# Norm factors put into the input rows before they are turned, with most turns behind the first products

## The chip, the cores and the metric

The kernel runs on one core of one Trainium2 chip. The metric is device time in microseconds (us) from the first to the last instruction of one execution, as a median of several runs; less is better. The engines are TensorE (PE in the profile; PEld is its weight load), VectorE (DVE), ScalarE (ACT), GpSimd (POOL) and SyncE (SP), which issues most transfers. A name with q (ACTq, SPq) is that engine's queue of DMA issues.

## The reference

One layer of a streaming encoder on 1024 prompt tokens and 32 sample tokens, width 1024: a SwiGLU feed-forward, a mix of two attention groups, a second SwiGLU. All inputs and outputs are 32-bit floats. What the change touches is the very beginning:

```python
def rms_norm(x, g):
    xf = x.astype(jnp.float32)
    y = xf * lax.rsqrt(jnp.mean(xf * xf, axis=-1, keepdims=True) + EPS)
    return (y * g.astype(jnp.float32)).astype(x.dtype)

def swiglu(x, w_in, w_out):
    a, b = jnp.split(x @ w_in, 2, axis=-1)
    return (jax.nn.silu(a) * b) @ w_out

x = x + 0.5 * swiglu(rms_norm(x, ffn1_norm), ffn1_w_in, ffn1_w_out)
```

`w_in` has 1024 rows and 2 x 2816 columns: a half for `a`, a half for `b`.

## The kernel before

Each 32-bit operand of a product is split into a high part (ScalarE, `split`, L158) and the rest that it leaves (VectorE, L159), and a product of two operands is three TensorE instructions per block of 128 rows: high by high, high by rest, rest by high. The names end in h and l: `B110h`, `B110l`; weights are `wh`, `wl`. The feed-forward is computed by Strassen's scheme with seven products per column block j of the weights, so sums of weights (`S1` to `S4`, `rS` before their split) and sums of tokens (`T1` to `T4`, `B11`, `B22`) are needed. The 1056 tokens stand in two groups c, of 256 and 272 in each half of the tokens; tiles 0, 1, 4, 5 of the input belong to c = 0, tiles 2, 3, 6, 7 and the sample's 8 to c = 1.

The input comes as tiles of 128 tokens by 1024 features (`xt`; `Tile`), and the products need features on the partitions, so each tile is turned, in two halves of four blocks. It is turned twice: once plainly, to be stored in a DRAM tensor `xf` for later (`raw`, L830; a copy `st` by ScalarE, L855, then a store), and once with its norm factor. For the factor, ScalarE squares and sums a tile (L815, into a spare buffer), GpSimd computes r from the sum (L817, L818), VectorE scales the identity by r into `dg` (L820), and TensorE multiplies the tile by `dg` (`normed`, L832). VectorE multiplies the result by the norm's gain g1 into `xn` (L843, L847 for the sample).

`early_products` then computes, for the first six column blocks (j = 0 to 5; `EARLY`), the two of the seven products that need only unsummed operands: for j = 0 and 1 first with c = 0, then with c = 1, and from j = 2 on both for each j. Their results go through `e` (L411 ScalarE, L413 VectorE) into a DRAM tensor `pd`, by stores that ScalarE issues. Between these groups it calls `amid(n)`, which holds turns, saves and preparations: `prep_first` and `prep_rest` (L383 and splits) build the token operands. A column's weights are split when the last product that reads their buffer is done.

The main loop (`first_products`) goes through all j; for j < 6 it has five products left and fetches the two others from `pd` (`p1`, and `gt` on which ScalarE then does a SiLU, L573). During one j, it loads the next j's weights, sums and splits them. SyncE and ScalarE's queue carry the loads; the stores of a finished j are `td` and `gd`.

A scheduler of the language sets the order of instructions on each engine by the order of the code, by readiness and by priorities; each engine then works its list in order. Where the code says `behind(g, ...)`, it adds an order after the named instructions. The first stretch of the program is that of TensorE's 72 plain turns, 144 records of turns by `dg`, and the early products of j = 0 and 1.

## Time and profile before

| | us |
|---|---|
| median of 3 runs | 2148.93 |
| lowest and highest | 2145.74, 2150.28 |
| the profiled execution | 2150.68 |
| its span, first to last instruction | 2149.0 |
| TensorE busy | 2107.0 |
| TensorE's first instruction | 7.64 |
| first early product | 19.10 |
| first product of j = 2 | 50.26 |
| first product of the main loop | 73.68 |

The profile is that of one execution. In the timeline a row has the start in us, the duration, engine, line, operation, output <- input, the number of instructions run together (x16), and in brackets the idle time of the engine before it with what ended that. In the groups, a row has the busy time, the mean of one in ns, and the idle time before. Duration of TensorE rows overlaps: the distance of two starts is what one costs. In the windows a row has the busy time of PE, PEld, DVE, ACT and POOL, with counts, then the granted TensorE clock (1.00 is full), the share of the DMA engines, and GB/s.

### The profile page before, as it was taken

To read this page: it belongs to the slowest core of one execution; us is meant where nothing else is said; L and a number is where in the kernel's file an instruction comes from. 1 tells how busy PE (TensorE), PEld (TensorE's weight loads), DVE (VectorE), ACT (ScalarE), POOL (GpSimd) and SP (SyncE) were. 2 spreads that over 40 slices of the span, in tenths; PEclk is the share of its full clock that TensorE was granted. 3 is DMA by queue.
4 is the path that set the end of the run, shared out by engine and by line. 5 is a ranking of instruction groups with operands and counts; after the bars stand their busy time and mean duration, and the time that the engine had idled before them with its cause. 6 is when DMAs were issued, how large, how long until landed. Compare 5 with 4: busy or idle time off the path is not lost. (4 is left out here: it accounts for less than half of the span.)

```text
span 2149.0 us, 41522 instructions
## 1 busy us (share of the span) xinstructions
PE 2107.0 (98%) x16331; PEld 2053.9 (96%) x16331; DVE 1471.8 (68%) x2559; ACT 936.1 (44%) x1830; POOL 582.7 (27%) x873
## 2 busy tenths in 40 slices
PE   8999999999999999999999999999999999999999
PEld 7999999999999999999899898999999999999998
DVE  6777666664678568778678688559767666645775
ACT  6433333333446555555564575246223233334443
POOL 1355544441000111311311311031555454320000
PEclk9999999999999999999999999999999999999999
DMA  7665454547635310120111223465765555567343
GB/s 241 189 212 169 151 179 151 165 145 261 214 125 173 102 57 21 48 67 21 61 54 30 67 62 96 143 196 165 218 214 169 168 163 163 167 224 238 119 145 126
DMA packets 327364, 305.12 MB, mean 142 GB/s; under 512 B 26432, under 2 KB 283200, under 8 KB 327168
## 3 DMA queue, kind: packets, MB, share of 16 engines
q1 hardware_dynamic: 258016, 262.59, 37.7%
q10 hardware_dynamic: 68672, 38.25, 6.3%
q8 instruction: 128, 2.10, 0.4%
q0 software_dynamic: 480, 1.62, 0.2%
q14 instruction: 68, 0.56, 0.1%
HBM read 207.37 MB, written 95.03 MB: 141 GB/s over the span
## 5 line engine op out<-in xcount | busy, mean ns | idle before, releaser
L776 PE MATMUL bk<-tl,wh 128*128 128x256 f32 x1144 | 324.9, 285 | 2.0 <-DVE tl L733 1.9
L776 PE MATMUL bk<-th,wh 128*128 128x256 f32 x1144 | 322.7, 284 | 0.7 <-ACT th L732 0.7
L776 PE MATMUL bk<-th,wl 128*128 128x256 f32 x1144 | 322.1, 282 | 0.0
L915 PE MATMUL pp<-xs_a,wh 128*128 128x384 f32 (+1 forms) x1008 | 258.5, 338 | 0.0
L776 PEld LDWEIGHTS bk<-tl,wh 128*128 128x128 f32 x1144 | 214.8, 188 | 2.9 <-DVE tl L733 2.8
L776 PEld LDWEIGHTS bk<-th,wl 128*128 128x128 f32 x1144 | 215.6, 188 | 0.2 <-issue 0.2
L776 PEld LDWEIGHTS bk<-th,wh 128*128 128x128 f32 x1144 | 213.9, 188 | 1.2 <-ACT th L732 1.0
L915 PEld LDWEIGHTS pp<-xs_a,wh 128*128 128x128 f32 x1008 | 168.5, 189 | 6.0 <-issue 4.1
L915 PE MATMUL pp<-xs_a,wl 128*128 128x384 f32 (+1 forms) x504 | 163.9, 325 | 0.0
L601 POOL TENSOR_TENSOR gt<-gt,b 128x256 f32<-128x256 f32 x88 | 72.9, 829 | 310.8 <-ACT gt L600 306.6
L718 DVE SCALAR_TENSOR_TENSOR wl<-oraw,wh 128x1024 fp32r<-128x1024 f32 x78 | 89.9, 1152 | 94.6 <-ACT wh L717 94.6
L600 ACT ACTIVATE gt<-gt 128x256 f32<-128x256 f32 x88 | 37.2, 423 | 231.0 <-DVE gt L568 230.8
L717 ACT ACTIVATE wh<-oraw 128x1024 fp32r<-128x1024 f32 x78 | 77.7, 996 | 134.6 <-PE bk L776 115.2
L159 DVE TENSOR_TENSOR wl<-wraw,wh 128x512 fp32r<-128x512 f32 (+2 forms) x126 | 112.9, 911 | 26.8 <-ACT wh L158 25.9
L431 PE MATMUL bk<-ops_a,wh 128*128 128x256 f32 (+1 forms) x704 | 130.2, 285 | 0.7 <-ACT e L411 0.6
L158 ACT ACTIVATE wh<-wraw 128x512 fp32r<-128x512 f32 (+2 forms) x126 | 89.4, 731 | 79.4 <-PE bk L431 27.2
L431 PEld LDWEIGHTS bk<-ops_a,wh 128*128 128x128 f32 x704 | 108.8, 188 | 1.6 <-ACT e L411 1.4
L605 POOL TENSOR_TENSOR gt<-gt,b 128x256 f32<-128x256 f32 x88 | 87.0, 989 | 72.0 <-DVE b L568 59.1
L431 PE MATMUL bk<-ops_a,wl 128*128 128x272 f32 (+1 forms) x352 | 99.9, 285 | 0.4 <-DVE wl L159 0.3
L568 DVE TENSOR_TENSOR b<-bk,u 128x272 f32<-128x272 f32 (+1 forms) x176 | 75.2, 427 | 34.8 <-PE bk L431 20.8
L568 DVE TENSOR_TENSOR gt<-bk,p 128x256 f32<-128x256 f32 (+1 forms) x60 | 25.9, 432 | 104.5 <-PE bk L431 101.9
L915 PEld LDWEIGHTS pp<-xs_a,wl 128*128 128x128 f32 x504 | 94.7, 188 | 0.1
(444 smaller groups left out, 6674.8 us busy)
## 6 DMA issues: line engine op xcount, KB each, us to landing
wraw<-in_ffn_w_in_dram SPq DMA_DIRECT2D x58, 512.0 KB, 4.2
oraw<-in_ffn_w_out_dram SPq DMA_DIRECT2D x94, 256.0 KB, 4.6
sd<-osum SPq DMA_DIRECT2D x44, 512.0 KB, 3.2
gd<-gt SPq DMA_DIRECT2D x42, 528.0 KB, 5.0
braw<-in_ffn_w_in_dram ACTq DMA_DIRECT2D x42, 512.0 KB, 4.4
oraw<-sd SPq DMA_DIRECT2D x40, 512.0 KB, 3.7
oraw<-in_ffn_w_out_dram SPq DMA_DIRECT2D x30, 512.0 KB, 3.9
wraw<-in_w_in_dram SPq DMA_DIRECT2D x28, 512.0 KB, 3.7
```

The costliest lines, as they stand in the source:

```text
L158: nc.scalar.activation(hi, src, AF.Copy)
L159: return nc.vector.tensor_tensor(out=lo, in0=src, in1=hi, op=ALU.subtract)
L431: mm = g.nc.tensor.matmul(ps, wt[x][:, kk, :], xt[y][:, kk, :], start=(first and kk == 0 and n == 0), stop=(kk == HK - 1 and n == len(PASS ...
L568: add = lambda out, other: nc.vector.tensor_tensor(out=out, in0=ps, in1=other, op=ALU.add)
L600: silu = nc.scalar.activation(gt[:, 1, cc], gt[:, 1, cc], AF.Silu)
L601: nc.gpsimd.tensor_tensor(out=gt[:, 1, cc], in0=gt[:, 1, cc], in1=s["b2"], op=ALU.mult)
L605: last = nc.gpsimd.tensor_tensor(out=gt[:, 0, cc], in0=gt[:, 0, cc], in1=s["b1"], op=ALU.mult)
L717: nc.scalar.activation(h, r, AF.Copy, scale=0.5)
L718: nc.vector.scalar_tensor_tensor(out=l, in0=r, scalar=0.5, in1=h, op0=ALU.mult, op1=ALU.subtract)
L776: nc.tensor.matmul(ps, wt[a][:, d * P:(d + 1) * P], xt[b][:, cols(c)], start=(k == 0 and n == 0), stop=(k == FH - 1 and n == len(PASSES) - 1))
L915: g.filler = nc.tensor.matmul(ps[:, 0:gw(n)], wt[a][:, k, :], xs(b, k)[:, gs(n)], start=(k == 0 and j == 0), stop=(k == KC - 1 and j == le ...
```

## The change

Five things are changed, all in the first feed-forward's opening.

1. The factor r no longer goes into the identity. `Tile.scaled` multiplies the tile's rows by r into a new tile `xr`, as two halves, on ScalarE (L829) for tiles 1, 3, 5, 7 and on VectorE (L831) for tiles 0, 2, 4, 6, 8. The turn of `xr` is then the same plain turn by the identity as that of the raw tile.
2. The order of the code is another. Tiles 0 and 1 are turned, then the products of j = 0 follow at once; tiles 2, 3 and 8 are turned after the first two products (`amid(0)`), 4 and 5 after the third pair (`amid(2)`), 6 and 7 after the fourth (`amid(3)`, behind `prep_rest`). The squares are issued earlier than the turns.
3. The first rows are fetched before the constants, and the load of g1 comes after the first weights.
4. The buffers: nine for `xt`, `ss` and `r`.
5. In the main loop, the first column's weights are loaded by GpSimd's queue into buffers of their own (`araw`, and `braw`), in `amid(3)`, and no longer by SyncE into the shared buffer.

```diff
+    def load_a(self, j, raw=None):
+        queue = self.g.nc.sync if raw is None else self.g.nc.gpsimd
+        if raw is None:
+            raw = self.g.wp.tile([P, KC, P], F32, name="wraw", tag="wraw", bufs=2)
+        queue.dma_start(raw, self.v[:, :, j * P:(j + 1) * P])
...
     def factor(self, spare):
...
-        self.dg = pool.tile([P, P], F32, name="dg", tag="dg", bufs=4)
-        nc.vector.tensor_scalar(out=self.dg[0:R, 0:R], in0=g.ident[0:R, 0:R], scalar1=r[0:R, 0:1], scalar2=None,
-                                op0=ALU.mult)
-
-    def turned(self, h, m):
+
+    def scaled(self):
+        nc, R, r = self.g.nc, self.R, self.r
+        self.xr = self.pool.tile([P, D], F32, name="xr", tag="st", bufs=6)
+        for h in range(2):
+            cs = slice(HD * h, HD * h + HD)
+            out, src = self.xr[0:R, cs], self.xt[0:R, cs]
+            if self.tt in (1, 3, 5, 7):
+                nc.scalar.activation(out, src, AF.Copy, scale=r[0:R, 0:1])
+            else:
+                nc.vector.tensor_scalar(out=out, in0=src, scalar1=r[0:R, 0:1], scalar2=None, op0=ALU.mult)
+
+    def turned(self, h, rows):
...
-            if m is None:
-                nc.tensor.transpose(pn[:, k, 0:R], src, self.g.ident[0:R, 0:R])
-            else:
-                nc.tensor.matmul(pn[:, k, 0:R], src, m[0:R, 0:R], start=True, stop=True)
+            nc.tensor.transpose(pn[:, k, 0:R], rows[0:R, (4 * h + k) * P:(4 * h + k + 1) * P], self.g.ident[0:R, 0:R])
...
+    fetch_rows(0, 1)
+    first_consts(g, const, w)
...
     def amid(n):
-        if n == 1:
+        if n == 0:
+            with behind(g, firsts[1]):
+                norm_rows(2, 3, 8)
+            factor_rows(4, 5)
+        elif n == 1:
             prep_first(g, None, None, None, xs[1], xns[1])
             save_rows(8, 0, 1)
+            factor_rows(6, 7)
+        elif n == 2:
+            norm_rows(4, 5)
+            save_rows(2, 3)
         elif n == 3:
-            save_rows(2)
-            norm_rows(4, 5)
-            save_rows(3, 4, 5)
-            for tt in (6, 7):
-                rows[tt].factor(spare)
             prep_rest(g, None, None, None, xs[0], xns[0])
-            for tt in (6, 7):
-                rows[tt].normed(xns)
-            save_rows(6, 7)
+            norm_rows(6, 7)
+            save_rows(4, 5, 6, 7)
             lds.close()
             g.a1s, a1 = pool_of("f1a")
             wts.lay_out(a1)
+            g.rs, rp = pool_of("f1r")
+            wts.load_a(0, rp.tile([P, KC, P], F32, name="araw"))
+            wts.load_b(0, nc.gpsimd)
         elif n == 7:
             with behind(g, g.power, g.landed):
-                start_weights(wts)
-
-    fetch_rows(0, 1)
+                start_weights(wts, True)
+
     wts.load_a(0)
+    g.g1 = col(g, const, "g1", w["ffn1_norm"].rearrange("o (c p) -> p (o c)", p=P), KC)
     fetch_rows(2, 3, 8)
+    wts.load_a(1)
+    factor_rows(0, 1)
     norm_rows(0, 1)
     wts.split_a(0)
-    prep_first(g, None, None, None, xs[0], xns[0])
-    wts.load_a(1)
-    norm_rows(2, 3, 8)
+    factor_rows(2)
+    firsts = prep_first(g, None, None, None, xs[0], xns[0])
+    with behind(g, firsts[0]):
+        factor_rows(3, 8)
     fetch_rows(4, 5)
     wts.load_a(2)
     fetch_rows(6, 7)
```

How the scheduler's order moves is seen best on ScalarE. Below are its instructions around the split of the third column's weights (`wh_402` before, `wh_427` now). `e1` are results of early products, `st` saved plain turns, `pd0` and `xf0` stores. Before:

```order
L411 ACTIVATE e1_383<-bk_370 128x272
L855 ACTIVATE st_356<-bk_363 128x512
L158 ACTIVATE wh_402<-wraw_247 128x512 x2
L858 DMA xf0_62<-st_356 1024x1x128
L411 ACTIVATE e1_423<-bk_410 128x272
```

And now:

```order
L412 ACTIVATE e1_408<-bk_395 128x272
L865 DMA xf0_62<-st_357 1024x1x128
L157 ACTIVATE wh_427<-wraw_205 128x512 x2
L862 ACTIVATE st_371<-bk_372 128x512
L862 ACTIVATE st_371<-bk_378 128x512
L416 DMA pd0_68<-e1_408 128x272
L865 DMA xf0_62<-st_371 1024x1x128
L416 DMA pd0_68<-e2_424 128x272
L829 ACTIVATE xr_450<-xt_203,r_303 128x512 x2
L862 ACTIVATE st_465<-bk_466 128x512
```

The scaled rows of tile 5 (`xr_450`) stand behind the split `wh_427`, two saves and three DMA issues; before, no turn waited for ScalarE here. On VectorE the scaled rows of tile 4 stand behind `e2_424` and the two `wl_428`.

The second place is the split of the fourth column's weights and the operands of `prep_rest`. Before:

```order
L855 ACTIVATE st_530<-bk_537 128x512
L815 ACTIVATE T40h_112,ss_551<-xt_251 128x1024
L858 DMA xf0_62<-st_530 1024x1x128
L158 ACTIVATE B220h_111<-xn0_104 128x1024
L158 ACTIVATE T10h_109<-xn0_104 128x1024
L158 ACTIVATE T30h_110<-xn0_104 128x1024
L855 ACTIVATE st_596<-bk_597 128x512
```

And now:

```order
L865 DMA xf0_62<-st_479 1024x1x128
L157 ACTIVATE wh_525<-wraw_215 128x512 x2
L416 DMA pd0_68<-e2_522 128x272
L157 ACTIVATE B220h_95<-xn0_88 128x1024
L157 ACTIVATE T10h_93<-xn0_88 128x1024
L157 ACTIVATE T30h_94<-xn0_88 128x1024
L829 ACTIVATE xr_562<-xt_209,r_392 128x512 x2
L157 ACTIVATE T20h_92<-xn0_88 128x1024
L862 ACTIVATE st_577<-bk_578 128x512
```

Before, tile 7's square (`ss_551`) stood ahead of the three splits; now its square is long done, and its scaled rows (`xr_562`) stand behind them.

The third place is in the main loop, where the splits of the weights of j = 3 begin (`S2h_1500` before, `S2h_1513` now). L573 and L576 are SiLUs of what was fetched from `pd`, L600 and L603 other SiLUs. Before:

```order
L573 ACTIVATE gt1_1498<-gt1_1498 128x256
L158 ACTIVATE S2h_1500<-rS2_1454 128x512
L600 ACTIVATE gt0_1285<-gt0_1285 128x256
L573 ACTIVATE gt1_1498<-gt1_1498 128x272
L158 ACTIVATE S1h_1519<-rS1_1453 128x512
```

And now:

```order
L157 ACTIVATE S2h_1513<-rS2_1467 128x512
L576 ACTIVATE gt1_1511<-gt1_1511 128x256
L603 ACTIVATE gt0_1298<-gt0_1298 128x256
L576 ACTIVATE gt1_1511<-gt1_1511 128x272
L157 ACTIVATE S1h_1532<-rS1_1466 128x512
```

`S2h` has moved ahead of the SiLU of the fetched piece; `S1h` still stands behind both. From about 150 us of the program on, the order on each engine is the same as before.

More of the change, by code (lines that the diff above doesn't have):

```diff
@@ L366, in prep_first @@
 def prep_first(g, xc, rr, gain, xs, dst):
+    done = []
     for h, o in enumerate(FIRST_OPERANDS):
@@ L371, in prep_first @@
                 scaled(g.nc.vector, dst[:, k, 0], xc[:, k, 0], gain, rr[:, 0], k)
-        split(g.nc, *xs[o], dst[:, h * HK:h * HK + HK, 0, :])
+        done.append(split(g.nc, *xs[o], dst[:, h * HK:h * HK + HK, 0, :]))
+    return done
 def prep_rest(g, xc, rr, gain, xs, dst):
@@ L448, in lay_out, with load_b @@
             self.first[n] = tile_w(pool, [P, HK, P], n, n, 1)
-    def load_a(self, j):
-        raw = self.g.wp.tile([P, KC, P], F32, name="wraw", tag="wraw", bufs=2)
-        self.g.nc.sync.dma_start(raw, self.v[:, :, j * P:(j + 1) * P])
+    def load_a(self, j, raw=None):
[3 more added lines that the diff above has]
+        queue.dma_start(raw, self.v[:, :, j * P:(j + 1) * P])
         self.raw[j] = [raw, None]
-    def load_b(self, j):
+    def load_b(self, j, queue=None):
         if j == 0:
@@ L458, in load_b @@
         raw = self.pool.tile([P, KC, P], F32, name="braw", tag="braw", bufs=1)
-        queue = self.g.nc.scalar if j else self.g.nc.sync
+        queue = queue or (self.g.nc.scalar if j else self.g.nc.sync)
         queue.dma_start(raw, self.v[:, :, FF + j * P:FF + (j + 1) * P])
@@ L807, in __init__ @@
         R = self.R
-        tag, bufs = ("xt", 8) if tt < 8 else ("st", 6)
-        self.xt = pool.tile([P, D], F32, name="xt", tag=tag, bufs=bufs)
+        self.xt = pool.tile([P, D], F32, name="xt", tag="xt", bufs=9)
         g.landed = nc.sync.dma_start(self.xt[0:R], src)
@@ L813, in factor @@
         g, nc, pool, R = self.g, self.g.nc, self.pool, self.R
-        ss = pool.tile([P, 1], F32, name="ss", tag="ss", bufs=3)
+        ss = pool.tile([P, 1], F32, name="ss", tag="ss", bufs=9)
         nc.scalar.activation(spare[0:R], self.xt[0:R], AF.Square, accum_out=ss[0:R])
-        r = pool.tile([P, 1], F32, name="r", tag="r", bufs=3)
+        r = self.r = pool.tile([P, 1], F32, name="r", tag="r", bufs=9)
         nc.gpsimd.tensor_scalar(out=r[0:R], in0=ss[0:R], scalar1=1.0 / D, scalar2=EPS, op0=ALU.mult, op1=ALU.add)
         g.power = nc.gpsimd.tensor_tensor(out=r[0:R], in0=r[0:R], in1=g.mh[0:R], op=ALU.pow)
-        self.dg = pool.tile([P, P], F32, name="dg", tag="dg", bufs=4)
-        nc.vector.tensor_scalar(out=self.dg[0:R, 0:R], in0=g.ident[0:R, 0:R], scalar1=r[0:R, 0:1], scalar2=None,
-                                op0=ALU.mult)
-    def turned(self, h, m):
+    def scaled(self):
[9 more added lines that the diff above has]
+    def turned(self, h, rows):
         nc, R = self.g.nc, self.R
@@ L836, in normed @@
         g, tt = self.g, self.tt
+        self.scaled()
         for h in range(2):
-            pn = self.turned(h, self.dg)
+            pn = self.turned(h, self.xr)
             ks = slice(4 * h, 4 * h + 4)
@@ L854, in raw @@
         for h in range(2):
-            nc.scalar.activation(st[:, 4 * h:4 * h + 4, 0:R], self.turned(h, None), AF.Copy)
+            nc.scalar.activation(st[:, 4 * h:4 * h + 4, 0:R], self.turned(h, self.xt), AF.Copy)
         if tt < 8:
@@ L1699, in tile_layer, with start_weights @@
     g.wp = ctx.enter_context(tc.tile_pool(name="wp", bufs=2, reuse_waits="tile"))
-    first_consts(g, const, w)
     g.slabs = Slabs(g, g.wp, slabs_of(w["w_in"], mix_cols)
                     + [[wo[:, 0:3, d * P:(d + 1) * P], wo[:, 4:7, d * P:(d + 1) * P]] for d in range(KC)])
-    def start_weights(wts):
-        wts.load_a(0)
-        wts.load_b(0)
+    def start_weights(wts, loaded=False):
+        if not loaded:
+            wts.load_a(0)
+            wts.load_b(0)
         wts.sums(0)
@@ L1726, in fetch_rows, with factor_rows @@
             rows[tt] = Tile(g, w, ldp, psp, tt)
+    fetch_rows(0, 1)
+    first_consts(g, const, w)
+    def factor_rows(*tts):
+        for tt in tts:
+            rows[tt].factor(spare)
     def norm_rows(*tts):
         for tt in tts:
-            rows[tt].factor(spare)
             rows[tt].normed(xns)
@@ L1737, in amid @@
     def amid(n):
-        if n == 1:
+        if n == 0:
[3 more added lines that the diff above has]
+        elif n == 1:
             prep_first(g, None, None, None, xs[1], xns[1])
             save_rows(8, 0, 1)
+            factor_rows(6, 7)
+        elif n == 2:
+            norm_rows(4, 5)
+            save_rows(2, 3)
         elif n == 3:
-            save_rows(2)
-            norm_rows(4, 5)
-            save_rows(3, 4, 5)
-            for tt in (6, 7):
-                rows[tt].factor(spare)
             prep_rest(g, None, None, None, xs[0], xns[0])
-            for tt in (6, 7):
-                rows[tt].normed(xns)
-            save_rows(6, 7)
+            norm_rows(6, 7)
+            save_rows(4, 5, 6, 7)
             lds.close()
@@ L1772, in tile_layer @@
     n0s.close()
+    g.rs.close()
     x1s, x1p = pool_of("f1x1")
```

2 lines of the change are left out of this document (removed).

## The prediction

> **What bounds the kernel now.** I read the page first, then the waits of TensorE (PE), then its timeline over the first 130 us, with the other engines' timelines beside each gap.
>
> ```profile
> span 2149.0 us, 41522 instructions
> ...
> PE 2107.0 (98%) x16331; PEld 2053.9 (96%) x16331; DVE 1471.8 (68%) x2559; ACT 936.1 (44%) x1830; POOL 582.7 (27%) x873
> ```
>
> TensorE sets the end: 2107.0 of 2149.0 us, so only 42 us of idle time are left in the whole program. A change at the start can do three things: take work off TensorE, remove some of its idle time, or add some. The waits name what there is to remove (engine, what waited for what: total, times, longest):
>
> ```profile
> PE bk L431 <- DVE S2l L159: 2.9, 8, 1.1
> ...
> PE bk L832 <- ACT B220h L158: 2.6, 1, 2.6
> PE bk L431 <- ACT S2h L158: 2.4, 3, 1.5
> ```
>
> The rest of what matters is the wait of 7.64 us before the first instruction. Idle time has a second price here. In the stretches below the columns are the busy time of each engine with its instruction count, then the granted clock:
>
> ```profile
> 7.50:12.25 4.75, 4.61 (x21) 4.61 (x22) 2.95 (x6) 3.52 (x8) 1.52 (x5) 1.00 1.09 373
> 12.25:22.00 9.75, 9.75 (x85) 9.59 (x84) 8.16 (x16) 7.09 (x11) 2.92 (x8) 1.00 0.68 257
> 46.50:50.00 3.50, 3.50 (x19) 3.50 (x18) 3.50 (x4) 1.28 (x3) 0.91 (x1) 0.52 0.88 198
> 90.75:94.25 3.50, 3.50 (x16) 3.50 (x17) 3.50 (x7) 0.00 (x0) 2.52 (x4) 0.51 0.16 55
> ```
>
> At full clock TensorE does one instruction per 9.75/85 = 0.115 us. In the two stretches at clock 0.5 it does 19 and 16 in 3.5 us, where 30 fit: 11 and 14 instructions short, so 1.3 to 1.6 us lost, I take 1.4. The first 4.75 us are as slow (0.22 us each), though the clock column shows 1.00 there. Each half-clock stretch follows a gap of over 2 us. So a gap of 2 us costs about 3.4.
>
> **The change part by part.** The stretch that is rewritten:
>
> ```profile
> 7.64 11.53 PE L832 MATMUL bk<-dg,xt 128*128 128x128 f32 x80 [7.64 <-DVE dg L820]
> 19.10 0.39 PE L431 MATMUL bk<-B110h,wh 128*128 128x256 f32 x1
> ...
> 21.94 0.28 PE L431 MATMUL bk<-B210h,wl 128*128 128x256 f32 x1
> ...
> 27.31 0.49 PE L431 MATMUL bk<-B11s,wh 128*128 128x272 f32 x2
> ...
> 33.41 1.04 PE L830 MATMUL bk<-identr,xt 128*128 128x128 f32 x8
> ...
> 37.86 2.78 PE L830 MATMUL bk<-identr,xt 128*128 128x128 f32 x24
> 40.48 1.95 PE L832 MATMUL bk<-dg,xt 128*128 128x128 f32 x16
> 45.07 2.50 PE L832 MATMUL bk<-dg,xt 128*128 128x128 f32 x16 [2.64 <-ACT B220h L158]
> 47.36 3.14 PE L830 MATMUL bk<-identr,xt 128*128 128x128 f32 x16
> 50.26 0.36 PE L431 MATMUL bk<-B110h,wh 128*128 128x256 f32 x1
> ```
>
> *Removed.* A turn by a matmul with the scaled identity `dg` leaves 16 records per tile (1.95 us); a plain turn leaves 8 (24 in 2.78: 0.93 us a tile). Nine tiles save 72 x 0.117 = 8.4 us of TensorE work. Those of tiles 2, 3 and 8 also leave the path to the first product.
>
> *Start, up to the first products.* Rows of SyncE, ScalarE, GpSimd and VectorE:
>
> ```profile
> 0.80 0.46 SPq L42 DMA_DIRECT2D g<-in_ffn_norm_dram  x1
> ...
> 5.18 1.06 ACT L815 ACTIVATE T40h<-xt 128x1024 fp32r<-128x1024 f32 x1 [3.10 <-DMA xt<-in_x_prompt_dram]
> ...
> 6.49 1.06 ACT L815 ACTIVATE T40h<-xt 128x1024 fp32r<-128x1024 f32 x1 [0.16 <-DMA xt<-in_x_prompt_dram]
> ...
> 6.42 0.19 POOL L817 TENSOR_SCALAR r<-ss 128x1 f32<-128x1 f32 x1 [5.05 <-ACT T40h L815]
> 6.69 0.58 POOL L818 TENSOR_TENSOR r<-r,mh 128x1 f32<-128x1 f32 x1
> ...
> 9.19 1.23 DVE L159 TENSOR_TENSOR wl<-wraw,wh 128x1024 fp32r<-128x1024 f32 x1 [0.31 <-ACT wh L158]
> 10.34 0.68 DVE L843 TENSOR_TENSOR xn<-bk,g 128x512 f32<-128x512 f32 x1
> ...
> 15.65 1.20 DVE L159 TENSOR_TENSOR B110l<-xn,B110h 128x1024 fp32r<-128x1024 f32 x1
> ```
>
> The gain's load moves behind the first rows, which are then issued 0.5 us earlier: squares from 4.7 and about 6.0. GpSimd now computes the factor of tile 1 before it raises tile 0's to its power, so r of tile 0 waits for the second square: 6.0 + 1.24 (square to r, 5.18 to 6.42) + 0.2 + 0.6 gives 8.05. The new scaled rows on VectorE are an operation that the trace has only in other widths:
>
> ```profile
> L1352 DVE TENSOR_SCALAR hf<-hf,olb,lb 128x384 f32<-128x384 f32 x8 | 3.8, 476 | 1.4 <-ACT hf L1350 1.1
> ...
> L158 ACT ACTIVATE wh<-wraw 128x512 fp32r<-128x512 f32 x76 | 45.8, 628 | 35.6 <-PE pp L915 25.2 <-PE bk L431 5.7 <-PE bk L776 4.6
> ...
> 34.15 1.29 DVE L159 TENSOR_TENSOR wl<-wraw,wh 128x512 fp32r<-128x512 f32 x2 [1.72 <-ACT wh L158]
> ...
> 21.25 0.37 ACTq L415 DMA_DIRECT2D pd<-e  x1
> ...
> 44.59 1.04 ACT L158 ACTIVATE T10h<-xn 128x1024 fp32r<-128x1024 f32 x1
> ```
>
> 128x512 must lie between 0.48 (its 384 columns) and 0.68 (the tensor-tensor of 512); I take 0.55, near the first, since it has one stream of input. ScalarE's half is a copy of 512, 0.63 (0.54 apart). Then: scaled rows 0 at 8.1 to 9.1, VectorE's wl 1.23 (to 10.3), four gain products 0.6 apart (tile 1's from 11.5), B110h from 12.2, B110l to 14.5. TensorE has issued two products by then; the 22 others run from 14.5, at 0.117 to 17.1, at the half clock of a start to 18.9: I take 18.0. Before, this group ended at 22.0. **4.0 us earlier** (3.1 to 4.9).
>
> *Next group.* Tiles 2 and 3 turn to 19.9. Tile 8's scaled rows stand on VectorE behind the sum e2 of the first products and behind four gain products of tiles 2 and 3; the last of these ends at about 20.9, so TensorE waits 1.5 us. Then tile 8, 24 products (2.85), 24 raw turns (2.8) and 24 products of width 272 (6.10/2 = 3.05): **31.0**. The kernel before had at 33.4 all this and 24 products (3.05) more; the lead of 4.0 is now -0.6: the wait (1.5) and the turns of tiles 2, 3 and 8 (2.8), which no longer lie ahead of the first product, have eaten it.
>
> *Stall at rows 4 and 5.* The scaled rows 4 stand on VectorE behind e2 and the weights' wl, those of 5 on ScalarE behind wh, two saved pieces and three DMA issues; wh may start only when the product that reads its buffer is done, at 31.0. wh 0.63, wl twice 0.6, one scaling 0.55: TensorE idles **2.35 us**. Its half clock costs 1.4 more, and the turn of 5, ready at 35.3, hides in that. After 16 raw turns and 24 products: 31.0 + 2.35 + 1.87 + 1.4 + 1.87 + 3.05 = 41.5.
>
> *Stall at row 7.* Its scaled rows stand on ScalarE behind wh twice (1.2), a pd issue (0.37) and the three splits B220h, T10h, T30h (0.95 apart): 41.5 + 1.2 + 0.35 + 2.9 + 0.6 = 46.6, while tile 6 keeps TensorE busy to 42.4: **4.1 us** idle, against 2.64 now. Then 40 turns, 3.5 us of them at half clock: 40 x 0.117 + 1.4 = 6.1, so the third column of weights begins at about **52.7**, against 50.26: **2.4 us later**. Both ends: 1.0 later if the clock does not fall after the 2.35 us gap; 5.7 later if it falls after the 1.5 us gap too, the start runs at half clock to its end, and raw 7, whose bank waits for a saved piece behind T20h on ScalarE, waits 1 us more.
>
> The Trainium skill ("TensorE: Matmul & The Clock Gate", Part 1, "What's actually happening") says that the clock falls after an idle window of about 3.4 us that runs freely. By that, only the 4.1 us gap would pay and the third column would begin 1.4 us sooner. The trace disagrees: 2.64 us and less of idle time were each followed by 3.5 us at 0.5.
>
> *Main loop.* Its first weights now come by GpSimd's queue, before 40 us; in the trace TensorE does not wait for them at the loop's start, so this buys nothing. The first gap there stays: VectorE must pass p1, six sums and four weight sums before S2l, in the same number. The second is this:
>
> ```profile
> 114.17 0.45 SPq L626 DMA_DIRECT2D gd<-gt  x1
> ...
> 117.29 0.80 SPq L557 DMA_DIRECT2D gt<-pd  x2
> ...
> 122.65 0.42 ACT L573 ACTIVATE gt<-gt 128x256 f32<-128x256 f32 x1 [10.39 <-DMA gt<-pd]
> ...
> 123.64 0.39 PE L431 MATMUL bk<-T20h,S2h 128*128 128x256 f32 x1 [1.48 <-ACT S2h L158]
> ```
>
> S2h stood behind a SiLU that waited for gt. In the changed order S2h comes first, and the store gd, for which gt's load waits, comes before td, some 1.5 us sooner. 2.1 us of idle time and 1.4 of half clock go: **-3.5** (0 if S1h, still behind that SiLU, now waits instead).
>
> Sum: +2.4 - 3.5, and +0.5 for raw 7's wait, half of its bound: -0.6 us. The profiled execution took 2150.68, so 2150.1; it lay 1.75 above the median, so on the median's scale 2148.3. The 8.4 us of work saved are given back by idle time: TensorE waits for B110l at the start (from about 11.3, when tile 1 is turned, to 14.5), for tile 8, for rows 4 and for rows 7.
>
> **The rivals.** *Slower.* One mechanism: scaled rows wait in order on ScalarE and VectorE, TensorE idles over 2 us three times, and each time half clock follows; +5.7 at the third column, and gt's load lands no sooner, so the loop repays nothing: 2148.9 + 5.7 = 2154.6. For it: each term is an exact order with measured durations. It decides from the point where the SiLU's load is as late against the loop as now. Chance 0.22.
>
> *Faster.* The stalls at rows 4 and 7 come out shorter (1.0 later at the third column), and both gaps of the loop go, 3.5 and 2.6 + 1.4: 1.0 - 7.5 = -6.5, 2142.4. For it: 8.4 us of TensorE work are really gone, and the first gap of the loop depends on one load, p1, that SyncE may issue a little earlier. Against it: T2s's splits, which hold p1 back, keep their place. Chance 0.27.
>
> *Swallowed.* The loop absorbs any shift of its start in its own waits. Against it: TensorE is 98% busy, so a shift passes on. It ends within the same bound, and is counted there.
>
> **How the numbers follow.** About 0.2% (4.3 us) is what a measurement can tell here from no change. No change 0.51, faster 0.27, slower 0.22. The likeliest case's own range is 2145 to 2152; with the two others' ends, 2141.5 to 2155.
>
> **What would show it.** First products at 13 to 15 us; a wait of TensorE for tile 8's rows, one of about 2.3 us for rows 4 near 32, one of about 4 for rows 7 near 42 to 47, each of the last two followed by half clock; the third column at 52 to 54; no gap of 2 us at the fourth column of the loop (before at 122). Wrong if the third column begins before 50, or if the loop's second gap stays.

## The result and the profile after

The changed kernel takes 2163.5 us, the median of 4 runs (2161.06 to 2167.52); the kernel before took 2149.61 in 4 runs on the same chip. The ratio is 1.0069, with an interval of 1.0048 to 1.009: it is slower, by some 14 us. The forecast was 2148.3 and no change. The profiled execution of the changed kernel:

```profile
span 2160.9 us, 41389 instructions
...
PE 2102.9 (97%) x16259; PEld 2047.9 (95%) x16259; DVE 1475.4 (68%) x2560; ACT 942.1 (44%) x1838; POOL 586.2 (27%) x875
```

The plain turns did remove TensorE work: 72 instructions fewer, 4.1 us less busy time. The idle time grew from 42.0 to 58.0 us, and part of the busy time that is left runs at half clock, so that the 8.4 us expected from the instruction count are only half visible (the mean granted clock is 0.995, before it was 0.998). TensorE's timeline in the opening and the first columns of the loop shows where it idles (start, duration, what runs, and in brackets the idle time before it with what ended it):

```profile
15.20 0.39 PE L432 MATMUL bk<-B110h,wh 128*128 128x256 f32 x1 [3.32 <-ACT B110h L157]
...
20.35 1.91 PE L838 MATMUL bk<-identr,xr 128*128 128x128 f32 x16
24.00 0.79 PE L838 MATMUL bk<-identr,xr 32*128 32x32 f32 x8 [1.74 <-DVE xr L831]
...
37.25 1.06 PE L838 MATMUL bk<-identr,xr 128*128 128x128 f32 x8 [2.41 <-DVE xr L831]
39.02 1.27 PE L838 MATMUL bk<-identr,xr 128*128 128x128 f32 x8 [0.71 <-ACT xr L829]
...
50.27 1.97 PE L838 MATMUL bk<-identr,xr 128*128 128x128 f32 x8 [4.35 <-ACT xr L829]
...
57.17 0.66 PE L838 MATMUL bk<-identr,xt 128*128 128x128 f32 x4 [1.73 <-ACT st L862]
59.44 0.66 PE L838 MATMUL bk<-identr,xt 128*128 128x128 f32 x4 [1.62 <-ACT st L862]
59.85 0.36 PE L432 MATMUL bk<-B110h,wh 128*128 128x256 f32 x1
...
84.72 0.28 PE L432 MATMUL bk<-T20h,S2h 128*128 128x256 f32 x1
...
102.90 0.39 PE L432 MATMUL bk<-T20h,S2h 128*128 128x256 f32 x1 [2.70 <-ACT S2h L157]
...
105.47 0.58 PE L432 MATMUL bk<-T20h,S2l 128*128 128x256 f32 x1 [0.89 <-DVE S2l L158]
```

The waits for scaled rows (tile 8, rows 4, 5 and 7) are the ones that the order had shown. The third column of weights (j = 2) begins at 59.85 us, 9.6 later than before (the recorded expectations below put it at 60.4); the loop begins at 84.72, 11.0 later. What the kernel before did not have, and the prediction had as 1 us at most, is the pair of waits of 1.73 and 1.62 us for saved pieces, at 57 and 59 us. The other engines' rows tell why, and what happens at the two ends of the opening:

```profile
2.82 4.11 SPq L812 DMA_DIRECT2D xt<-in_x_prompt_dram  x2
...
11.67 1.06 ACT L817 ACTIVATE T40h<-xt 128x1024 fp32r<-128x1024 f32 x1 [1.42 <-DMA xt<-in_x_prompt_dram]
...
14.10 1.04 ACT L157 ACTIVATE B110h<-xn 128x1024 fp32r<-128x1024 f32 x1
...
46.49 1.26 POOL L482 TENSOR_TENSOR rS<-braw 128x512 f32<-128x512 f32 x1 [4.11 <-DVE xn L850]
...
51.07 2.25 POOL L485 TENSOR_TENSOR rS<-araw,rS 128x512 f32<-128x512 f32 x1
...
46.73 3.25 DVE L158 TENSOR_TENSOR wl<-wraw,wh 128x512 fp32r<-128x512 f32 x2
49.90 2.29 DVE L158 TENSOR_TENSOR B220l<-xn,B220h 128x1024 fp32r<-128x1024 f32 x1
52.12 2.29 DVE L158 TENSOR_TENSOR T10l<-xn,T10h 128x1024 fp32r<-128x1024 f32 x1
...
55.57 1.06 ACT L157 ACTIVATE T20h<-xn 128x1024 fp32r<-128x1024 f32 x1 [4.74 <-DVE xn L384]
...
90.51 3.69 DVE L158 TENSOR_TENSOR T2s<-xn,T2s 128x1088 fp32r<-128x1088 f32 x3
...
94.22 0.34 SPq L559 DMA_DIRECT2D p<-pd  x1
```

- *At the start* ScalarE squares tile 2 (11.67) and tile 3 (to 14.1) ahead of the split B110h, and it waits 1.42 us for tile 2's rows, whose issue with those of tile 3 took 4.11 us.
- *At 46 to 54 us* GpSimd's four weight sums run beside VectorE's splits. Part 5 brought three of them here; before, only the first ran here, and the others at 62.59 to 68.24. B220l and T10l take 2.29 us each, where a split of this size with no sum beside it took 1.20 to 1.23 (before, B220l took 1.64 beside the one sum and T10l 1.21). So T20h waits 4.74 us, the two saved pieces behind it are late, and TensorE waits for the buffers `bk` that they empty.
- *In the loop* the last of the T2s splits ends at 94.20, 9.5 us after the loop's start, and the first fetch from `pd` is issued at 94.22. Before, it was issued at 79.31, 5.6 after the loop's start.

The same place before, and TensorE's two waits in the loop's first gap, which were 1.85 us there (VectorE, SyncE, TensorE):

```profile
46.85 1.64 DVE L159 TENSOR_TENSOR B220l<-xn,B220h 128x1024 fp32r<-128x1024 f32 x1
...
79.31 0.34 SPq L556 DMA_DIRECT2D p<-pd  x1
...
89.16 0.39 PE L431 MATMUL bk<-T20h,S2h 128*128 128x256 f32 x1 [0.77 <-ACT S2h L158]
...
90.75 0.53 PE L431 MATMUL bk<-T20h,S2l 128*128 128x256 f32 x1 [1.08 <-DVE S2l L159]
```

The half clock, seen in windows (busy time of PE, PEld, DVE, ACT, POOL with counts, then the granted clock, DMA share, GB/s) behind the waits at 24.0, 37.25, 50.27 and 59.4:

```profile
24.00:29.00 5.00, 5.00 (x32) 4.75 (x32) 3.45 (x7) 4.29 (x7) 2.13 (x6) 0.70 0.07 26
37.25:42.25 5.00, 4.29 (x35) 3.86 (x36) 4.07 (x7) 2.82 (x5) 0.77 (x1) 1.00 1.10 324
50.25:53.75 3.50, 3.48 (x19) 3.48 (x20) 3.50 (x2) 0.58 (x1) 3.07 (x2) 0.57 0.53 155
60.65:67.65 7.00, 7.00 (x48) 7.00 (x48) 3.54 (x5) 2.56 (x6) 0.00 (x0) 0.79 0.73 224
```

It followed the wait of 1.74 us, and not that of 2.41.

### The profile page after: what moved, and what is told of

Same layout as the page of the kernel before. It is cut to its first block, busy times and chain, and to the rows that moved or that the text cites. A ratio compares the mean times of both kernels' runs of the same rounds, so it can differ in the third digit from the quotient of the medians.

```text
span 2160.9 us, 41389 instructions
## 1 busy us (share of the span) xinstructions
PE 2102.9 (97%) x16259; PEld 2047.9 (95%) x16259; DVE 1475.4 (68%) x2560; ACT 942.1 (44%) x1838; POOL 586.2 (27%) x875
## 5 line engine op out<-in xcount | busy, mean ns | idle before, releaser
L603 ACT ACTIVATE gt<-gt 128x256 f32<-128x256 f32 x88 | 37.2, 423 | 225.2 <-DVE gt L571 225.0
```

Of the source, the lines that this page charges most:

```text
L603: silu = nc.scalar.activation(gt[:, 1, cc], gt[:, 1, cc], AF.Silu)
```

## The experiments

Every median stands against that of the kernel before, measured on the same chip beside it. The ratio is that of the means of the runs, so it is not quite that of the two medians. "Loop" is the start of the main loop, "second part" the first product `th` by `wh` (behind the loop), both in the profiled execution and as the distance to the kernel before (73.68 and 496.33 us). For the changed kernel these are +11.0 and +13.7. A profiled execution lies up to 3.8 us from its kernel's median (before_two_scaled: 2150.09 against 2153.84), so these two columns do not add up to the medians.

| kernel | us | before | ratio (interval) | loop | second part |
|---|---|---|---|---|---|
| the change | 2163.5 | 2149.61 | 1.0069 (1.0048 to 1.009) | +11.0 | +13.7 |
| g1_first | 2161.0 | 2148.33 | 1.0056 (1.0041 to 1.0072) | +9.2 | +12.0 |
| loop_weights_sync | 2158.69 | 2148.33 | 1.0047 (1.0032 to 1.0062) | +6.2 | +11.7 |
| scaled_rows_only | 2157.42 | 2148.33 | 1.0049 (1.0034 to 1.0065) | +11.1 | +11.1 |
| rows67_ahead | 2153.22 | 2148.33 | 1.0023 (1.0011 to 1.0034) | +4.9 | +7.7 |
| scaled_identity | 2156.77 | 2147.46 | 1.0042 (1.0027 to 1.0057) | +2.3 | +7.0 |
| rows67_and_sync | 2156.34 | 2147.46 | 1.0046 (1.003 to 1.0062) | +5.0 | +9.3 |
| rows45_early | 2154.04 | 2147.46 | 1.0035 (1.0022 to 1.0048) | +3.7 | +5.9 |
| before_pool_weights | 2153.27 | 2147.46 | 1.0025 (1.0015 to 1.0034) | -0.5 | +3.5 |
| order_alone | 2152.44 | 2148.28 | 1.0022 (1.0013 to 1.0031) | +2.4 | +3.1 |
| before_early_factors | 2155.1 | 2148.28 | 1.0027 (1.0017 to 1.0036) | +0.3 | +3.9 |
| before_two_scaled | 2153.84 | 2148.28 | 1.0023 (1.0014 to 1.0031) | +0.3 | +0.5 |
| sums_later | 2154.35 | 2149.31 | 1.0034 (1.0022 to 1.0047) | +5.1 | +7.5 |
| before_late_operands | 2150.9 | 2149.41 | 1.0003 (0.9994 to 1.0012) | +2.0 | +2.4 |

The intervals are up to 0.2% to either side, so two variants less than some 4 us apart are not told apart by their medians; the readings below rest on rows where that is so. No variant is faster than the kernel before.

**Parts undone in the changed kernel.** The gain's load first again:

```diff
+    g.g1 = col(g, const, "g1", w["ffn1_norm"].rearrange("o (c p) -> p (o c)", p=P), KC)
     fetch_rows(0, 1)
     first_consts(g, const, w)
     wts.load_a(0)
-    g.g1 = col(g, const, "g1", w["ffn1_norm"].rearrange("o (c p) -> p (o c)", p=P), KC)
```

> The changed kernel with one line moved: the load of the gain g1 is again the first on SyncE's queue, ahead of the rows. Theory (queue): in the changed kernel the issue of tiles 2 and 3 took 4.11 us on SyncE, because g1's many small packets stand ahead of them, so squares 2 and 3 ended at 12.8 and 14.2 us and B110h, which stands behind them on ScalarE, began at 14.10 where I had reckoned 12.2. Then here the issue takes about 1.1 us, B110h begins near 12.6, and the third column begins about 2 us before 60.4; the total falls by 2 to 3 us to about 2161. Rival (order): the lead is used up in the waits for tile 8 and rows 4, and the third column begins within 0.5 us of 60.4, total unchanged at 2163.5.

The rows of tiles 2 and 3 were issued in 1.25 us, not 4.11, and the first product came at 13.70, against 15.20. The waits for rows 4 and 7 (2.41, 4.66) and for saved pieces (1.25, 1.62) stayed, and the ratio is inside the changed kernel's interval. The rival held: the third column began at 59.52, only 0.3 us sooner. Rows 4 came 1.95 us sooner, but half clock followed them here (23 records in 5 us, where the changed kernel has 35), and rows 7 were waited for 0.31 longer. The issue of tiles 2 and 3 goes with the place of the gain's load: 3.32 to 4.11 us in the eight kernels that have the load just ahead of it, 1.09 to 1.25 in the seven that have it first. But a long issue alone does not make the start late: in loop_weights_sync it took 3.96 us, and the first product came at 13.66. In the eight kernels the first product came at 13.7 to 16.0; what sets it within that stays open.

Part 5 undone:

```diff
-            wts.load_a(0, rp.tile([P, KC, P], F32, name="araw"))
-            wts.load_b(0, nc.gpsimd)
...
-                start_weights(wts, True)
+                start_weights(wts)
```

> The changed kernel with part 5 undone: the main loop's first weights are loaded by SyncE into the shared buffer, late, as before. Theory (contention): GpSimd's four weight sums at 46.5 to 53.3 us slowed VectorE's wl pair (3.25 us instead of 1.29), B220l and T10l (2.29 each instead of 1.21), 4.1 us in all, so T20h and the saves behind it came late and TensorE waited 1.73 and 1.62 us at raw 7. Then without these sums there VectorE's splits take 1.2 to 1.3 us again, the two waits at raw 7 shrink below 1 us together, the third column begins near 57, and the total falls by 3 to 4 us to about 2160. Rival (order alone): T20h is late because of the order of the splits, the waits stay, third column at 60, total unchanged; or the sums only move and collide with VectorE later, and the total is unchanged though the third column begins earlier.

The splits B220l and T10l took 1.22 us each, no saved piece was waited for, and the loop began 4.8 us sooner than in the changed kernel. But the second part came only 2.0 sooner: the sums now ran at 73.51 to 80.59, at the loop's start, where its first weights and the T2s splits wait. TensorE's rows:

```profile
95.87 0.79 PE L432 MATMUL bk<-T2s,A22h 128*128 128x272 f32 x2 [2.50 <-DVE u L571]
...
103.01 0.39 PE L432 MATMUL bk<-T20h,S2l 128*128 128x256 f32 x1 [1.64 <-DVE S2l L158]
```

The slowdown of the splits is thus tied to part 5, but two things of part 5 were undone here at once, the queue and the time of the sums. A later run keeps the early queue and delays the sums alone, by a one-column copy on GpSimd that has to wait for tile 7's last gain product:

```diff
+        if loaded:
+            nc.gpsimd.tensor_scalar(out=wts.sums_of["S1"][:, 0, 0:1], in0=xns[1][:, 7, 1, 255:256], scalar1=1.0, scalar2=0.0,
+                                    op0=ALU.mult, op1=ALU.add)
         wts.sums(0)
```

> The changed kernel, with one thing added: GpSimd's four sums of the first column's weights wait for the last gain product of tile 7 (a one-column GpSimd copy of that product's result ahead of them), so that they no longer run beside VectorE's splits. The weights still come by GpSimd's queue before 42 us, and the order of instructions on the other engines is that of the changed kernel. Theory (GpSimd's sums and VectorE's splits slow each other): the sums start at about 61 us instead of 46.5; VectorE's wl, B220l and T10l take 0.65, 1.21 and 1.21 us each instead of 1.6, 2.29 and 2.29; the two waits for saved pieces before the third column (1.73 and 1.62) go to below 0.5 each, and that column begins near 57 instead of 60.4. The loop's first gap stays over 2 us, since the order there is the same. Median 2.5 to 4 us below the changed kernel. Rival 1 (the early queue and buffers, not the sums, delay the splits): VectorE's splits stay at 2.29 us although no sum runs beside them, time as the changed kernel. Rival 2 (the wait moves on): the splits are short, but the loop's start gains under 1 us because the early products of j = 2 to 5 wait for stores of e instead; time as the changed kernel.

Its timeline, rows of VectorE, GpSimd and TensorE:

```profile
46.87 1.22 DVE L158 TENSOR_TENSOR B220l<-xn,B220h 128x1024 fp32r<-128x1024 f32 x1
...
57.43 2.35 POOL L482 TENSOR_TENSOR rS<-braw 128x512 f32<-128x512 f32 x1
59.85 1.29 POOL L483 TENSOR_TENSOR rS<-rS,araw 128x512 f32<-128x512 f32 x1
...
62.10 2.54 DVE L158 TENSOR_TENSOR wl<-wraw,wh 128x512 fp32r<-128x512 f32 x2 [3.06 <-ACT wh L157]
...
49.34 1.73 PE L838 MATMUL bk<-identr,xr 128*128 128x128 f32 x8 [4.47 <-ACT xr L829]
50.86 4.86 PE L838 MATMUL bk<-identr,xt 128*128 128x128 f32 x32
55.47 0.36 PE L432 MATMUL bk<-B110h,wh 128*128 128x256 f32 x1
```

The splits are back at 1.22, the 32 raw turns run without a wait, and the third column begins at 55.47. From the turn of rows 7 to there it is 6.13 us, against 9.58 in the changed kernel: the 3.45 us are the two waits (3.35 together). The loop begins 5.9 sooner; 1.5 of that is the half clock that no longer follows them (48 instructions in 7 us at 60.65 above, where full clock gives 61), and 0.9 was there before any sum ran. That 1.5 is in part luck: in g1_first the waits of 1.25 and 1.62 were followed by full clock (57 records in the 7 us from 59.0, at 1.00). The median falls by more than foretold; the ratio is 1.0034, with an interval that only just lies apart from the changed kernel's. Where the delayed sums now meet other work, both are slow again (2.35 for a sum that takes 1.29 alone, 2.54 for `wl` that took 1.29). The Trainium skill ("SBUF — State Buffer", "SBUF: two separate sides") says that a VectorE operation with two inputs in SBUF and a GpSimd operation that reads SBUF share a pair of ports which the first to come holds for its whole instruction. The changed kernel's trace agrees in the main: alone, three VectorE steps (1.29, 1.22, 1.22) and four sums of 1.29 are 8.9 us; together they took from 46.49 to 54.41, 7.9, which is 1.0 less than strict turns would take.

**Scaled rows and scaled identity.** The scaled rows alone, in the kernel before with its order:

```diff
-            pn = self.turned(h, self.dg)
+            pn = self.turned(h, self.xr)
```

> The kernel before with the scaled rows and plain turns alone (parts 1 and 4): the order of the code, the queues and the first weights stay. Theory (order and its waits made the change slow, not the scaled rows): the 8.4 us of TensorE work saved come through in part: tiles 0 to 3 and 8 are turned by about 17 us instead of 19.1, so the first product begins near 17 and the third column near 46 to 48, total 2144 to 2147. Rival (the scaled rows themselves are what costs, since the turns now wait for ScalarE and VectorE in order): the first product is not before 19, waits of 2 us or more appear at rows 4 to 7, total 2152 or more.

Three rows of TensorE's timeline, the waits for tile 8 and for rows 6 and 7:

```profile
20.56 1.03 PE L836 MATMUL bk<-identr,xr 32*128 32x32 f32 x8 [2.03 <-DVE xr L829]
...
52.89 0.66 PE L836 MATMUL bk<-identr,xr 128*128 128x128 f32 x4 [2.53 <-ACT xr L827]
...
56.82 1.11 PE L836 MATMUL bk<-identr,xr 128*128 128x128 f32 x4 [3.27 <-ACT xr L827]
```

Nine tiles of cheaper turns, and the loop begins 11.1 us later. No GpSimd sum runs beside B220l and T10l here (1.23 us each), and the order of the code is that of before: the turns wait for ScalarE and VectorE at nine places after the first. By its median, 9.1 us, this is the change's largest single cost, and in this kernel the loop passes it on unchanged. The converse, the scaled identity in the changed order:

```diff
-            pn = self.turned(h, self.xr)
+            pn = self.turned(h, self.xt, self.dg)
```

> The changed kernel with part 1 undone: the order of the code, the queues and the buffers of the change, but the factor goes into the identity again (dg on VectorE, made with each factor) and the turns are matmuls by it. Theory (the scaled rows wait in order behind splits, and that made the change slow): the waits for scaled rows in the changed kernel (1.74 at tile 8, 2.41 and 0.71 at tiles 4 and 5, 4.35 at tile 7, and half clock behind them) vanish, though seven tiles then cost 6.5 us more of TensorE work; third column of weights 5 to 7 us before 60.4, total 2156 to 2159. Rival (the later turns themselves, whatever they are made of, hold up the splits): the third column stays at 60 or later and the total at 2163 or above.

Every wait for a turn behind the first is gone, and the loop begins 8.7 us sooner than in the changed kernel, though TensorE does its 72 instructions more. The second part comes 6.7 us sooner: the loop loses 4.7 us here against the kernel before, 2.7 in the changed kernel, and one wait in its first gap, 3.51 us, is the longest there in any of these kernels. TensorE's timeline at that wait (j = 1):

```profile
97.47 0.39 PE L432 MATMUL bk<-T20h,S2h 128*128 128x256 f32 x1 [3.51 <-ACT S2h L157]
```

**The order around rows 4 to 7.** Rows 6 and 7 scaled and turned ahead of the splits:

```diff
         elif n == 3:
-            prep_rest(g, None, None, None, xs[0], xns[0])
             norm_rows(6, 7)
+            prep_rest(g, None, None, None, xs[0], xns[0])
             save_rows(4, 5, 6, 7)
```

> The changed kernel with one call moved: the turns of tiles 6 and 7 ahead of prep_rest, so that the scaled rows 7 stand ahead of the splits B220h, T10h and T30h on ScalarE. Theory (order): the wait of 4.35 us at rows 7 falls to about 1.5 us, and no half clock follows it; if raw 7 does not wait longer in exchange, the third column begins 3 to 4.5 us sooner, total about 2159. Rival (contention): T20h and the saves are set by VectorE's slowed splits, so raw 7 waits the longer, the third column stays near 60 and the total at 2163.

TensorE's timeline at the turn of rows 7 and behind it:

```profile
49.05 1.27 PE L838 MATMUL bk<-identr,xr 128*128 128x128 f32 x8 [1.54 <-ACT xr L829]
50.15 3.66 PE L838 MATMUL bk<-identr,xt 128*128 128x128 f32 x32
```

The wait of 4.35 us is 1.54, and none for saved pieces follows: by its median, one moved line is worth more than half of the loss, and of the variants that keep all five parts this has the lowest ratio (1.0023). With part 5 undone as well:

> The changed kernel with two edits together: the turns of tiles 6 and 7 ahead of prep_rest, and the main loop's first weights by SyncE as before. Alone, the first gave 2153.2 and the second 2158.7, against 2163.5. Theory (contention is a cost of its own): the sums leave VectorE's splits alone, and the main loop's start comes at about 74 to 76 us; total 2148 to 2150. Rival (both edits took away the same wait, raw 7 behind T20h): the second adds nothing, the loop starts at 78.5 and the total stays at 2153; or, with the sums at 73 to 80 us as in the second edit alone, they collide with VectorE inside the loop and give back what was gained.

The two gains do not add: the loop began as in rows67_ahead. The sums ran at 70.7 to 79.4 us, and TensorE's waits in the loop went on. With rows 6 and 7 ahead, and rows 4 and 5 scaled as soon as their factors are there:

```diff
             rows[tt].factor(spare)
+            if tt in (4, 5):
+                rows[tt].scaled()
```

> The changed kernel with the turns of 6 and 7 ahead of prep_rest, and besides the scaled rows 4 and 5 made right behind their factors, ahead of the split of the third column's weights. Theory (order): the wait of 2.41 us at rows 4 and of 0.60 at rows 5 is gone, and the half clock after it: third column and loop start 3 to 4.5 us sooner than with rows 6 and 7 alone (78.5), total about 2149. Rival (the time is owed by ScalarE and VectorE anyway): B11's splits, which now stand behind the scaled rows, come later, TensorE waits for them before the products of width 272, loop start within 1 us of 78.5, total 2153.

TensorE's timeline at the turn of rows 6:

```profile
46.20 1.94 PE L838 MATMUL bk<-identr,xr 128*128 128x128 f32 x8 [6.14 <-DVE xr L831]
```

No wait for rows 4 is left, but rows 6 are now waited for 6.14 us. The time owed to VectorE and ScalarE is paid at the next place where TensorE needs them, and the median is no better.

**Part 5 alone** in the kernel before (its two loads by GpSimd's queue, own buffers):

> The kernel before with part 5 alone: the main loop's first weights by GpSimd's queue into buffers of their own. Theory (contention): GpSimd's sums now fall among VectorE's splits of T10 to T40 at 45 to 57 us and slow each from 1.21 to about 2.29, 3 to 4 us in all; TensorE has only the early products of the third column to hide it, so loop start 0 to 3 us later than 73.7, total 2149 to 2152. Rival (the queue costs nothing, the collision of the changed kernel came from its order): loop start at 73.7, total within 1 us of the kernel before.

GpSimd's first sum, and TensorE's timeline at the loop's first gap (j = 1):

```profile
53.86 6.78 POOL L481 TENSOR_TENSOR rS<-braw 128x512 f32<-128x512 f32 x1 [5.29 <-PE bk L431]
...
92.62 0.39 PE L431 MATMUL bk<-T20h,S2h 128*128 128x256 f32 x1 [2.58 <-ACT S2h L158]
```

Neither the theory nor the rival had it: the total is above the 2149 to 2152 of the theory, the splits of the tokens took 1.22 us, the loop even began 0.5 sooner, and 4.0 us were lost in it. Here it was the sum that waited: it took 6.78 us, while VectorE's splits and sums of tokens beside it took 1.22 to 1.30 each; only a later split of weights, beside the last two sums, took 3.20 instead of 1.29. So which of the two engines waits differs from one order to the next. Part 5 costs 5.8 us here and 5.1 from order_alone to scaled_identity, in the one order in the loop's first columns, in the other with slow splits too (B220l 2.02, T10l 2.30 in scaled_identity).

**The order alone**, with the scaled identity and without part 5:

> The changed kernel with parts 1 and 5 undone: the turns by the scaled identity, the main loop's first weights by SyncE; what stays is the order of the code, the order of the first loads and the buffers. Theory (three costs that add): the scaled rows cost 6.7 us (2163.5 to 2156.8), the weights by GpSimd's queue about 5 (they did so on the kernel before, 2153.3 against 2147.5), so the order alone leaves 2150 to 2153, with a loop start near 76. Rival (the order itself is the cost, and the others only show in it): 2156 or more. A second rival (the order is a gain that the others hide): below 2146.

It costs 4 us. The three parts alone are 9.1 (scaled rows), 5.8 (part 5) and 4.2 (order), in sum 19; together they are 14. That waits overlap would explain the difference, but it is within what the intervals leave open.

**An earlier start in the kernel before.** First the factors of tiles 4 to 7 early, which removes the 2.64-us wait:

```diff
             save_rows(8, 0, 1)
+            for tt in (4, 5, 6, 7):
+                rows[tt].factor(spare)
```

> The kernel before with the squares and factors of tiles 4 to 7 made behind the saves of 8, 0 and 1, so that tile 7's factor is ready long before its turn; nothing else is changed. Theory (idle time at the start passes on to the end): the wait of 2.64 us at tile 7 and the half clock after it (1.4) go, loop start about 4 us before 73.7, total 4 us below the kernel before. Rival (swallowed): prep_rest's splits, now behind the third column's products on ScalarE, come later and hold the loop's own operands, loop start 4 us earlier but a longer gap at its second column; total unchanged.

TensorE's timeline, an early product of a later column and the loop's first gap:

```profile
65.23 0.39 PE L431 MATMUL bk<-B110h,wh 128*128 128x256 f32 x1 [1.82 <-ACT e L411]
...
93.82 0.39 PE L431 MATMUL bk<-T20h,S2h 128*128 128x256 f32 x1 [1.87 <-ACT S2h L158]
```

The wait and its half clock are gone, and 4 us are paid back at once: the later columns wait for `e` (1.82, 0.99, 1.20), so the loop starts no sooner, and its first gap is larger. The median is 6.8 us above the kernel before, more than the rival had, and the profile accounts for 3.9 of it by the second part. Then, on top of this, scaled rows for tiles 0 and 1 alone:

> The same with the scaled rows for tiles 0 and 1 alone, both on VectorE, where nothing stands ahead of them; the others are turned by the scaled identity. Theory (scaled rows pay where the engine that makes them is free): 16 records less in the half-clock start, first product at 17 to 17.5 instead of 19.1, total 1.5 to 2 us below the kernel with early factors. Rival: the two scalings put wl and the gain products 0.5 us later each, B110l comes no sooner, and nothing is gained over early factors.

TensorE stands 2.06 us before tile 2 instead, for its scaled identity, and the first product comes at 19.27, against 19.10: the cheaper turns of two tiles bring it no sooner, and the median differs from before_early_factors by less than their spread. So in these two runs an earlier wait removed, or cheaper turns, were not worth anything by themselves.

**The loop's first gap.** In every variant but scaled_rows_only it is larger than before and the first fetch from `pd` comes later against the loop's start (7.5 to 12.0 us after it, 5.6 before); the fetch always starts within 0.1 us of the end of the last T2s split. In scaled_rows_only the fetch came 3.6 us after the loop's start, and this column waited all the same (0.66, 0.75, 2.27), so a late fetch is not the only thing that makes a gap there. This run delays that end alone, in the kernel before, by doing the last low half three times more:

```diff
     prep_rest(g, None, None, None, xs[1], xns[1])
+    for _ in range(3):
+        g.nc.vector.tensor_tensor(out=xs[1]["T4"][1], in0=xns[1][:, HK:KC, 0, :], in1=xs[1]["T4"][0], op=ALU.subtract)
```

> The kernel before, with one addition: VectorE repeats the low half of the last token-operand split of c = 1 (T4, in T2s) three times, 3 x about 1.2 us, ahead of the main loop's first work; nothing else is added, and the values are the same. In every profile so far SyncE issues the first fetch of the early products (p, then gt) within 0.1 us of the end of the last T2s split on VectorE: 5.6 us after the loop's start in the kernel before, 9.5 after it in the changed kernel, and the gaps before j = 1 sum to 1.85 and 4.23 us. Theory (the changed order puts the T2s splits behind the weights' splits, the fetch of p and gt comes later against the loop, and that alone makes the first gap larger): here the fetch comes about 9.3 us after the loop's start, the gaps before j = 1 sum to 3.5 to 4.5 us, half clock follows, and the median lies 2 to 4.5 us above the kernel before. Rival (the larger first gap comes from another part of the changed order, such as the sums' place or the weights' queue): the fetch is late as said, but p and gt still land in time for the splits, the gap stays below 2.5 us, and the time is that of the kernel before within 1 us.

The timeline of VectorE (the added line), SyncE, TensorE and ScalarE:

```profile
80.73 3.93 DVE L1777 TENSOR_TENSOR T2s<-xn,T2s 128x1088 fp32r<-128x1088 f32 x3
...
84.72 0.34 SPq L556 DMA_DIRECT2D p<-pd  x1
...
93.96 0.39 PE L431 MATMUL bk<-T20h,S2h 128*128 128x256 f32 x1 [3.00 <-ACT S2h L158]
...
95.61 0.58 PE L431 MATMUL bk<-T20h,S2l 128*128 128x256 f32 x1 [1.15 <-DVE S2l L159]
...
124.12 0.62 ACT L158 ACTIVATE S2h<-rS 128x512 fp32r<-128x512 f32 x1
```

The fetch came 9.0 us after the loop's start (75.69), and the first gap grew to 4.44 us (0.29, 3.00, 1.15): the mechanism is as the theory says. Its price is not, there the rival was right: the time is that of the kernel before (1.0003, 0.9994 to 1.0012). In the profile the second gap, 1.48 and 0.23 us at 123.64 before, is gone with ScalarE's order unchanged (S2h still behind the SiLU, at 123.79), and from the loop's start to the second part only 0.4 us are lost. So the two gaps look like one debt, paid at one place or the other.

## Why the prediction was wrong

No change was forecast, and the kernel is slower, though the waits were mostly foreseen. Three terms of the sum failed: the start, which was mis-sized; part 5, which was put at nothing; and the -3.5 of the loop. The sum was -0.6 us; by the second part the trace has +13.7. Of the 14.3 between them, 3.8 are the start, 3.0 the raw turns (3.5, of which 0.5 was counted), 1.5 the half clock behind them, and 6.2 the loop; -0.2 is the rest. Against the trace of the changed kernel, step by step:

1. **Right: the waits that the order shows.** Tile 8: 1.5 foretold, 1.74 measured. Rows 4: 2.35 and 2.41. Rows 7: 4.1 and 4.35. From the turn of rows 4 to that of rows 7: 13.25 foretold, 13.02 measured; this agreement is in part luck, since the 13.25 held 1.4 of half clock that did not come here (35 records in the 5 us from 37.25), and did not hold the wait of 0.71 for rows 5, which was thought hidden. The new operation, estimated at 0.55 us, took 0.47 to 0.53 on VectorE. The signs named for being wrong did not come, the third column before 50 us or the loop's second gap staying; but the column, given as 52 to 54, came at 59.85.

2. **Wrong in size: the start.** "18.0" for the end of the first products was 20.35. B110h was reckoned at 12.2 and began at 14.10: the squares of tiles 2 and 3, which wait for their rows, stand ahead of it on ScalarE and were not costed. The other 0.4 us are mostly the half clock of the start, which held until about 19 us. A further 1.5 us went to half clock behind the wait for tile 8, which the working kept for its upper end. So TensorE stood for rows 4 at 34.84, not 31.0: 3.84 us.

3. **Wrong: part 5 "buys nothing" and costs nothing.** The prediction asked only whether TensorE waits for the loop's first weights. It did not ask what else the early landing lets run: GpSimd's sums, beside VectorE's splits. That raw 7 "waits 1 us more", of which half was taken, was 3.35; sums_later shows that it is 0 without that overlap. With 3.84, -0.2 (the 13.02) and 3.48 here (6.1 foretold, 9.58 measured), the third column is at 59.85 and not at 52.7. Half clock behind these waits took 1.5 more by the loop's start, +11.0.

4. **Wrong: "-3.5" in the loop.** The second gap did go, as foretold; the first did not stay. It grew from 1.85 to 4.23 us (0.44, 2.70, 0.20, 0.89), and the T2s splits, which the text says "keep their place", had lost it: all five of them, and two of the four sums of tokens that they read, now stand behind the loop's first weights' splits on VectorE (80.15 to 84.87); before, one of the five and three of the four sums stood ahead of these. before_late_operands shows that a later fetch makes the first gap larger, that in its kernel the two gaps cancel, and that S2h's new place, the reason given, is not needed for the second gap to go. By the second part the change had lost 2.7 more, where the prediction gained 3.5. What makes up this 2.7, which the variants show with 0 (scaled_rows_only) to 5.5 us (loop_weights_sync), was not settled; its cause stays open.

5. **The half clock.** "A gap of 2 us costs about 3.4" is no rule: a wait of 1.74 us was followed by half clock and one of 2.41 was not (0.70 and 1.00 above). In sums_later the same two waits had it the other way round:

```profile
23.25:28.25 5.00, 4.99 (x46) 4.72 (x47) 3.80 (x8) 4.73 (x9) 2.13 (x6) 1.00 0.09 30
35.00:40.00 5.00, 4.32 (x25) 4.08 (x26) 3.48 (x6) 1.75 (x3) 0.00 (x0) 0.66 1.04 306
```

The sentence of the Trainium skill that the prediction cited ("TensorE: Matmul & The Clock Gate", Part 1) has a window that runs freely; that the same wait is followed by either clock agrees with it. That about 3.4 us of idle time are needed does not: before, the waits of 0.77 and 1.08 us at 89.16 and 90.75, with two products between them, were followed by 3.5 us at 0.51.

6. **The rivals.** "Slower" named the mechanism that was there, scaled rows that wait in order on ScalarE and VectorE, and scaled_rows_only confirms it: 9.1 us by itself. Its price, 5.7, was too small by the terms of points 2 and 3, and by the loop's 2.7. Against "swallowed" stood that a shift passes on since TensorE is 98% busy; the loss of scaled_rows_only did pass on, while in before_early_factors a gain of 4 us in the opening was swallowed. The range, 2141.5 to 2155, left out what both unknown sizes could add.

## What to carry to other kernels

Where an operation moves from the engine that sets the end to two that feed it in order, the price is the order, not the duration: each scaled row took half a microsecond, and TensorE stood for it 0.7 to 4.4 us, while the scaling waited behind other work of its engine. A load that comes earlier should be followed to what it lets start, and to what that runs beside. And a gap removed in an opening can be worth little: the next wait along the chain has to be looked at too. In rows45_early, before_early_factors and loop_weights_sync later waits took more than half of it or all of it back; in rows67_ahead and sums_later most of it stayed.

## What the runs showed of the hardware that was not expected

- VectorE and GpSimd slow each other when both work on two 32-bit tensors in SBUF, and not always evenly: a 128x1024 split took 2.29 instead of 1.22 us, a 128x512 sum 2.35 instead of 1.29; in before_pool_weights a sum took 6.78 us while VectorE's steps beside it took 1.22 to 1.30.
- Half clock follows some waits of 1.74 us and not some of 2.41; the same wait differs between kernels that have the same instructions up to there.
- The issue of two tiles' rows on SyncE's queue took 0.88 us at the program's start and 4.11 behind the gain's load in the changed kernel, 1.25 in g1_first. The eight kernels with the load there have 3.32 to 4.11, the seven with the load first 1.09 to 1.25, one profile of each; what in the load does it is not shown.
